# One transformer block on one core: all eight late chunks of the modulation matrix summed by TensorE matvecs

## The chip, the cores and the metric

The kernel runs on one core of a Trainium2 chip. Five engines run their own instruction streams in order and meet by semaphores: TensorE (PE, with its weight loads shown as PEld), VectorE (DVE), ScalarE (ACT), GpSimd (POOL) and SyncE (SP), which here issues the transfers between HBM and SBUF. The metric is the device time of one execution in microseconds (us).

## The reference

One block on 256 tokens of width 1024: a modulation vector from `c`, a mixer (a gated delta rule with four heads and a chunked attention with eight), and a mixture of 32 experts, four per token.

```python
mod = jax.nn.silu(c) @ w_ada[l] + b_ada[l]                       # [1, 6*1024]
sh1, sc1, ga1, sh2, sc2, ga2 = [m[:, None, :] for m in jnp.split(mod, 6, axis=-1)]
h = rms_norm(x, norm_w[l, 0]) * (1 + sc1) + sh1
y = hybrid_mixer(h, w_in[l], ...)                                # delta rule, attention, w_out
x = x + ga1 * rms_norm(y, norm_w[l, 1])
h = rms_norm(x, norm_w[l, 2]) * (1 + sc2) + sh2
y = moe_ffn(h, w_router[l], b_router[l], w_up[l], b_up[l], w_down[l], b_down[l])
x = x + ga2 * rms_norm(y, norm_w[l, 3])
```

`w_ada` is 1024 x 6144. The change concerns the product of `silu(c)` with the columns of it that give `ga1`, `sh2`, `sc2` and `ga2`.

## The kernel before

**Stages.** The front stage (0 to about 254 us in the trace) computes the modulation, the projections, the delta rule, the attention, the output projection, the residual and the routing. The expert stage then goes through 14 groups of one, two or four experts; each group loads six blocks of 512 columns per expert (2 MB each) and multiplies them by gathered tokens. The weights of the experts are 402 MB and come through a ring of ten slots in SBUF (`wB`, `w0`, `wC`, `wE`, `w1`, `wD`, `wF`, `wh`, `wA`, `wx`). In the front stage the same memory holds the projection weights, the pieces of the delta rule and the late chunks.

**The modulation.** `w_ada` is cut in twelve chunks of 512 columns, each [128 partitions, 8 k, 512]. Four chunks (`sc1`, `sh1`) come first (`hpath`). The other eight are the late chunks: chunk i belongs to segment i // 2 (0 `ga1`, 1 `sh2`, 2 `sc2`, 3 `ga2`), half i % 2. `ADAPOS` says after which step of the work a chunk is loaded and reduced, `ADATAG` in which slot (`wF` or `wB`); in program order they are c0, c2, c4, c3, c6, c1, c5, c7 (c1 and c5 at the same step, c7 a step later). `ADA` holds a letter per chunk.

With "D" (six chunks: c0, c1, c3, c4, c6, c7) VectorE multiplies the eight k slices by `silu(c)` and adds them in place (L723 once, L725 seven times, 512 wide), and four matmuls against a column of ones (L728) sum over the partitions. With "P" (c2 and c5) TensorE does it all in `colvec`: eight matmuls whose stationary operand is one value of `silu(c)` per partition, spread over 32 columns (L196); four of them fill the four groups of 32 rows of a PSUM bank, the next four add to them. ScalarE copies the bank to SBUF (`ev`, L199), and four matmuls against the indicator `ind` (L201) sum the four groups. Either way VectorE then adds bias and norm weight (L733, L736). Both ways take a PSUM bank of the tag `tp`, of which there are two, shared with the transposes of the attention (L785) and others.

**What sets the order.** The source lists the work once; a scheduler orders each engine's instructions when the kernel is built, with the delta rule (`chain`, L486) marked as high priority, so a change of one line can move instructions on every engine. From L1043 on the order on TensorE and VectorE is as written. On SyncE the transfers go one after the other: one that waits holds all behind it.

**The delta rule.** `chain` inverts triangular blocks by five levels (L595 in `pair_mm`): a product, copies of it to SBUF (L626 on ScalarE, L627 on VectorE), two more products, subtractions on VectorE (L633, L637), and so on. Then come the joining of the two halves (L659, L662), and the passing of the state (L684 to L709), each step a few matmuls and copies (L654, L680). `level` (L586) makes the masks that the levels need; the first two are on VectorE (L588). The projections run in the order k, q, qb, kb, vb, v, z, each in two column halves of two heads (`stream`, L406). A column half needs its weight split in a rounded part and a rest (`split`, L205): ScalarE rounds (L217), VectorE and GpSimd subtract (L219, L222); TensorE then runs 24 matmuls of 256 columns per head (L232).

**After the front stage.** `delta_out` normalizes the delta rule's result (L884 squares on ScalarE, L888 on VectorE), L891 transposes it, and the output projection, the residual, the routing and the first gather follow.

Of the kernel before, what the change touches and what calls it, by code (L numbers as in the profile page):

```python
# [24 lines left out]
K2 = 4  # L25
K1 = 6
KV = 2
ADA = list("DDPDDPDD")
ADATAG = list("FFBFFFFB")
ADAPOS = [5, 31, 6, 12, 8, 31, 19, 32]  # L30
ADABANK = "tp"
# [18 lines left out]
def block_kernel(ctx, tc, x, small, rows, rel_ext, wpre, wexp, b_up, b_down, out,  # L50
# [22 lines left out]
    def bank(tag="mm"):  # L73
        return ps.tile([P, 512], F32, tag=tag, bufs=PB[tag], name=tag)
# [641 lines left out]
    def modrow(seg, hf, w):  # L716

        if ADA[2 * seg + hf] == "P":
            b_ = bank("tp")
# [682 lines left out]
```

## Time and profile before

| | |
|---|---|
| median of 3 runs | 1191.61 us (1190.53 to 1195.18) |
| profiled execution | 1192.22 us, span 1190.4 us |
| PE, DVE, ACT, POOL busy | 1029.8, 358.7, 190.3, 104.1 us |
| granted TensorE clock, mean | 0.953 |
| HBM read | 449.50 MB, 379 GB/s over the span |

In the tables of stretches each row gives the busy time of the engines in that stretch with the number of instructions, the granted clock of TensorE (1.00 is 2.4 GHz, 0.50 is 1.2 GHz), the busy share of the 16 DMA engines and the GB/s. In rows in order of time stand the start, the duration, the engine, the line, the operation and the tiles written and read; a bracket at the end gives the idle time of the engine before it and who ended it. TensorE's fp32 matmuls appear as two records each, those of the rounded type as one.

### The profile page before, as it was taken

What the parts mean: (1) busy time and instruction counts of PE and PEld (TensorE: products, weight loads), DVE (VectorE), ACT (ScalarE), POOL (GpSimd) and SP (SyncE); (2) the same over time, 40 slices, a digit from 0 to 9 for tenths busy, and PEclk for the clock granted to TensorE, in tenths of its full rate; (3) what the DMA queues carried; (4) which work ended last, traced back from release to release, by engine and by line L of the source; (5) the groups of instructions that cost most, each with busy time, mean ns of one, the idle gap of its engine ahead of it and who ended that gap; (6) DMA issues with size and microseconds to landing.
All of it is one profiled execution on the core that took longest, in us unless ns stands there. A gap on an engine that the chain in (4) does not pass through costs nothing. (4 is left out here: it accounts for less than half of the span.)

```text
span 1190.4 us, 14727 instructions
## 1 busy us (share of the span) xinstructions
PE 1029.8 (87%) x5845; PEld 495.3 (42%) x5845; DVE 358.7 (30%) x851; ACT 190.3 (16%) x380; POOL 104.1 (9%) x91
## 2 busy tenths in 40 slices
PE   4898999899977789999976788989967698998985
PEld 2697998654321224435421233335322142433331
DVE  5387888654103022122111012122201011111113
ACT  3453327331001001011000001011001001010101
POOL 1557514200000000000000000000000000000001
PEclk9899999989998999999997999999988899999998
DMA  9925346989999999999999999999999999999993
GB/s 362 403 81 213 142 178 237 401 353 386 421 421 422 421 408 426 423 428 423 423 422 424 427 425 426 424 427 425 420 426 425 423 427 423 426 426 422 428 419 149
DMA packets 51463, 451.93 MB, mean 380 GB/s; under 512 B 5760, under 2 KB 7424, under 8 KB 9408
## 3 DMA queue, kind: packets, MB, share of 16 engines
q1 hardware_dynamic: 51392, 450.97, 91.3%
q8 instruction: 47, 0.77, 0.3%
q14 instruction: 24, 0.20, 0.0%
HBM read 449.50 MB, written 1.05 MB: 379 GB/s over the span
## 5 line engine op out<-in xcount | busy, mean ns | idle before, releaser
L1123 PE MATMUL dl<-w_f,xg 128*64 128x512 f32 (+1 forms) x224 | 113.5, 653 | 9.7 <-DMA w_f<-in_wexp_dram 9.7
L1177 DVE TENSOR_TENSOR acc<-acc,mm 128x512 f32<-128x512 f32 x52 | 35.8, 688 | 242.2 <-PE mm L1172 242.2
L1123 PE MATMUL mm<-w_f,xg 128*64 128x512 f32 (+2 forms) x208 | 92.7, 594 | 4.0 <-DMA w_f<-in_wexp_dram 4.0
L1279 POOL TENSOR_TENSOR wF_f<-acc,m_row 128x512 f32<-128x512 f32 x3 | 3.8, 1273 | 943.1 <-DMA w_f<-in_wexp_dram 937.3
L1123 PE MATMUL dl<-wh,xg 128*64 128x512 f32 (+2 forms) x144 | 70.3, 633 | 5.1 <-DMA wh<-in_wexp_dram 5.1
L1123 PE MATMUL dl<-wD_f,xg 128*64 128x512 f32 (+1 forms) x128 | 65.4, 662 | 4.3 <-DMA wD_f<-in_wexp_dram 4.3
L1172 PE MATMUL mm<-yg,wts 128*128 128x512 f32 x112 | 54.5, 614 | 11.0 <-ACT yg L1169 10.0
L1141 ACT ACTIVATE sg<-gm 128x512 f32<-128x512 f32 x28 | 17.6, 630 | 288.9 <-DVE gm L1139 263.1
L1123 PE MATMUL dl<-wE_f,xg 128*64 128x512 f32 (+2 forms) x112 | 55.2, 645 | 6.4 <-DMA wE_f<-in_wexp_dram 6.4
L1123 PE MATMUL mm<-wB_f,xg 128*64 128x512 f32 (+2 forms) x128 | 57.6, 595 | 0.0
L1123 PE MATMUL mm<-wh,xg 128*64 128x512 f32 (+1 forms) x144 | 57.1, 594 | 0.5 <-DMA wh<-in_wexp_dram 0.5
L1123 PE MATMUL dl<-wF_f,xg 128*64 128x512 f32 (+2 forms) x112 | 54.5, 628 | 2.8 <-DMA wF_f<-in_wexp_dram 2.8
L1123 PE MATMUL dl<-wC_f,xg 128*64 128x512 f32 (+2 forms) x112 | 55.4, 638 | 1.4 <-DMA wC_f<-in_wexp_dram 1.4
L1003 PEld LDWEIGHTS tp<-oh,x 128*128 128x128 f32 x432 | 50.7, 192 | 13.2 <-issue 11.4
L1003 PE MATMUL tp<-oh,x 128*128 128x128 f32 x432 | 54.8, 279 | 0.7 <-ACT aT__3377 L1152 0.7
L1123 PE MATMUL mm<-wE_f,xg 128*64 128x512 f32 (+1 forms) x112 | 49.6, 595 | 3.9 <-DMA wE_f<-in_wexp_dram 3.9
L1169 ACT COPY yg<-dl 128x512 f32<-128x512 f32 x27 | 15.8, 585 | 224.8 <-PE dl L1123 224.8
L1123 PE MATMUL dl<-wB_f,xg 128*32 128x512 f32 (+1 forms) x96 | 47.7, 634 | 3.5 <-DMA wB_f<-in_wexp_dram 3.5
L1013 DVE TENSOR_SCALAR xg<-tp,mc,mc 128x128 f32<-128x128 f32 x52 | 19.6, 405 | 101.1 <-PE dl L1123 92.4
L1123 PE MATMUL mm<-wC_f,xg 128*64 128x512 f32 (+1 forms) x112 | 50.0, 594 | 0.0
L1123 PEld LDWEIGHTS dl<-w_f,xg 128*64 128x64 f32 (+1 forms) x224 | 28.2, 134 | 42.6 <-issue 25.7
L1139 DVE TENSOR_SCALAR gm<-dl 128x512 f32<-128x512 f32 x14 | 9.7, 692 | 119.5 <-PE dl L1134 119.5
(640 smaller groups left out, 2193.3 us busy)
## 6 DMA issues: line engine op xcount, KB each, us to landing
wh<-in_wexp_dram SPq DMA_DIRECT2D x57, 1024.0 KB, 24.7
w_f<-in_wexp_dram SPq DMA_DIRECT2D x26, 2048.0 KB, 26.1
wA_f<-in_wexp_dram SPq DMA_DIRECT2D x36, 1024.0 KB, 22.2
wF_f<-in_wexp_dram SPq DMA_DIRECT2D x36, 1024.0 KB, 29.7
wE_f<-in_wexp_dram SPq DMA_DIRECT2D x15, 2048.0 KB, 29.4
wC_f<-in_wexp_dram SPq DMA_DIRECT2D x15, 2048.0 KB, 27.0
wB_f<-in_wexp_dram SPq DMA_DIRECT2D x13, 2048.0 KB, 22.2
wD_f<-in_wexp_dram SPq DMA_DIRECT2D x13, 2048.0 KB, 34.2
```

The costliest lines, as they stand in the source:

```text
L1003: T.matmul(b_[:, k * 128:(k + 1) * 128], x2[:, a, half(n)][:, k * 128:(k + 1) * 128], oh[:, a], start=a == tiles[0], stop=a == tiles[-1])
L1013: V.tensor_scalar(xg[:, k], src, mc, sc, op0=ALU.mult, op1=ALU.add)
L1123: T.matmul(b_[i * n:(i + 1) * n, :], lhs[:, k, i * n:(i + 1) * n], w(k), start=k == 0, stop=last and k == 7)
L1139: V.tensor_scalar(gm, bs[0], 7.0, None, op0=ALU.min)
L1141: S.activation(sg, gm, AF.Sigmoid, scale=1.702)
L1169: S.copy(yg, b_)
L1172: T.matmul(cb, wt[:, a], yg, start=True, stop=True)
L1177: V.tensor_add(acc[:, a, sl], acc[:, a, sl], cb)
L1279: (V if a and n else G).tensor_mul(fin[:, 0, a, sl], acc[:, a, sl], m3_row[:, sl])
```

## The change

`ADA` becomes all "P". The six chunks that VectorE summed now go through `colvec` as c2 and c5 do. Nothing else is edited.

```diff
-ADA = list("DDPDDPDD")
+ADA = list("PPPPPPPP")
```

The branch that reads it (unchanged):

```python
if ADA[2 * seg + hf] == "P":
    b_ = bank("tp")
    colvec(w, csil, b_, ADABANK)
else:
    ac = w[:, 0, :]
    V.tensor_scalar(ac, ac, csil[:, 0:1], None, op0=ALU.mult)
    for k in range(1, 8):
        V.scalar_tensor_tensor(ac, w[:, k, :], csil[:, k:k + 1], ac, op0=ALU.mult, op1=ALU.add)
    b_ = bank("tp")
    for m in range(4):
        T.matmul(b_[:, m:m + 1], ac[:, m * 128:(m + 1) * 128], ones[:, 0:1], start=True, stop=True)
```

The order of the instructions moves in three places that matter below.

On VectorE, where the delta rule's first masks are made (L588; L580 makes their input, L219 are subtractions of weight splits, L723 and L725 a chunk's sum, L733 and L736 a chunk's last step), the order before is:

```order
L580 TENSOR_TENSOR wB_f<-wE_f 64x512 x2
L219 TENSOR_TENSOR w_r<-w_f,wh 128x512
L588 TENSOR_TENSOR Lm<-wB_f,lvm_249 128x512
L588 TENSOR_TENSOR Lm<-wB_f,lvm_258 128x512
L576 SCALAR_TENSOR_TENSOR wE_f<-dl,bb,m_incT 128x128 x4
L617 TENSOR_TENSOR wB_f<-id_231,Lm 128x512
L723 TENSOR_SCALAR wF_f<-wF_f,csil 128x512
L725 SCALAR_TENSOR_TENSOR wF_f<-wF_f,csil 128x512
L621 TENSOR_TENSOR wE_f<-id_231,dl 64x8x64 x2
```

and in the changed kernel:

```order
L580 TENSOR_TENSOR wB_f<-wE_f 64x512 x2
L733 SCALAR_TENSOR_TENSOR mc_946<-tp,sm 128x4
L733 SCALAR_TENSOR_TENSOR mc_1025<-tp,sm 128x4
L736 SCALAR_TENSOR_TENSOR mc_1025<-mc_1025,sm 128x4
L219 TENSOR_TENSOR w_r<-w_f,wh 128x512
L219 TENSOR_TENSOR w_r<-w_f,whx 128x512
L219 TENSOR_TENSOR w_r<-w_f,wh 128x512
L588 TENSOR_TENSOR Lm<-wB_f,lvm_249 128x512
L588 TENSOR_TENSOR Lm<-wB_f,lvm_258 128x512
L617 TENSOR_TENSOR wB_f<-id_231,Lm 128x512
```

The two masks now stand behind the last steps of c2 and c4 and behind the splits of the last three projection halves.

On TensorE, at the last levels of the delta rule (L595) and the joining of its halves (L659, L662; L232 with `wA_r` are projections, L761 the attention's scores, L785 its transposes), the order before is:

```order
L595 MATMUL dl<-wB_f 64x64 x24
L761 MATMUL mm<-wC_f 128x256 x2
L232 MATMUL mm<-wh,wA_r 128x256 x16
L232 MATMUL mm<-w_r,wA_r 128x256
L595 MATMUL dl<-wB_f 64x64 x8
L659 MATMUL dl<-wE_f 64x64 x8
L232 MATMUL mm<-w_r,wA_r 128x256 x7
L761 MATMUL mm<-wC_f 128x256 x4
L785 MATMUL tp<-ident,w_f 128x128 x4
L662 MATMUL dl<-wB_f 64x64 x4
L785 MATMUL tp<-ident,w_f 128x128 x3
L662 MATMUL dl<-wB_f 64x64 x4
```

and in the changed kernel, with L606 and L610 two transposes of the same chain:

```order
L761 MATMUL mm<-wC_f 128x256 x4
L595 MATMUL dl<-wB_f 64x64 x32
L606 MATMUL dl<-ident,kqT 128x128 x4
L610 MATMUL dl<-ident,wB_f 128x128 x4
L595 MATMUL dl<-wE_f,Lm 64x64 x16
L595 MATMUL dl<-wB_f 64x64 x32
L659 MATMUL dl<-wE_f 64x64 x8
L662 MATMUL dl<-wB_f 64x64 x8
L684 MATMUL dl<-wE_f 128x128 x4
L688 MATMUL dl<-wE_f,wB_f 128x128 x4
L692 MATMUL dl<-wE_f 128x128 x4
L696 MATMUL dl<-wE_f,kdt 128x128 x4
```

The projections and the attention's transposes no longer stand between the steps; the row goes on with L700, L703, L707 and L709, and the transposes (L785) begin behind them.

On TensorE, at the end of the first half of the output projection (L232 with `wC_r`) and ahead of L891, the order before is:

```order
L232 MATMUL mm<-wh,wC_r 128x512 x8
L232 MATMUL mm<-w_r,wC_r 128x512 x4
L196 MATMUL tp<-wF_f,csil 32x512 x8
L201 MATMUL tp<-ind,ev 128x1 x4
L728 MATMUL tp<-ones,wB_f 128x1 x4
L891 MATMUL tp<-ident,wE_f 128x128 x8
```

and in the changed kernel:

```order
L232 MATMUL mm<-w_r,wC_r 128x512 x4
L196 MATMUL tp<-wF_f,csil 32x512 x8
L201 MATMUL tp<-ind,ev 128x1 x4
L196 MATMUL tp<-wB_f,csil 32x512 x8
L201 MATMUL tp<-ind,ev 128x1
L891 MATMUL tp<-ident,wE_f 128x128 x4
L201 MATMUL tp<-ind,ev 128x1 x3
```

The sum of c7 (slot `wB`) is now eight matvecs with a copy behind them, in the place of the four matmuls against ones.

## Rows read from the trace of the kernel before

**Rows 1.** The page's 40 slices of the span, busy in tenths: three lines.
```profile
PE   4898999899977789999976788989967698998985
DVE  5387888654103022122111012122201011111113
DMA  9925346989999999999999999999999999999993
```

**Rows 2.** Stretches: length, PE, PEld, DVE, ACT, POOL busy, PEclk, DMA, GB/s.
```profile
87.50:112.00 24.50, 24.00 (x227) 22.28 (x226) 16.32 (x35) 12.00 (x19) 14.57 (x11) 1.00 0.46 172
112.00:124.00 12.00, 8.09 (x65) 7.48 (x63) 11.77 (x10) 3.01 (x4) 10.81 (x7) 0.72 0.48 176
124.00:172.00 48.00, 47.85 (x616) 46.17 (x616) 41.04 (x68) 10.77 (x18) 15.59 (x12) 1.00 0.42 155
172.00:204.00 32.00, 31.07 (x319) 26.57 (x318) 24.63 (x45) 20.25 (x61) 14.33 (x12) 1.00 0.67 264
...
215.20:221.20 6.00, 3.86 (x33) 2.27 (x32) 5.79 (x14) 0.74 (x2) 2.57 (x2) 0.98 1.03 419
...
290.00:1170.00 880.00, 766.64 (x3694) 286.77 (x3693) 149.81 (x313) 75.38 (x147) 0.00 (x0) 0.96 1.01 423
```

**Rows 3.** SyncE's waits, 180 to 300 us: waited for, total, times, longest.
```profile
SPq L1115 <- PE mm L1123: 17.4, 1, 17.4
SPq L81 <- PE tp L728: 12.9, 1, 12.9
```

**Rows 4.** The same columns as Rows 2, the stretch in which the ring was full.
```profile
260.00:262.00 2.00, 2.00 (x12) 0.78 (x13) 0.00 (x0) 0.40 (x1) 0.00 (x0) 1.00 0.00 0
```

**Rows 5.** SyncE in order of time: the load of c5.
```profile
205.14 0.33 SPq L81 DMA_DIRECT2D wF_f<-in_wpre_dram  x1
```

**Rows 6.** TensorE in order of time: c2, then the end of c5 and c7.
```profile
100.62 1.92 PE L196 MATMUL tp<-wB_f,csil 128*32 128x512 f32 x16
102.47 2.17 PE L232 MATMUL mm<-wA_r,wh 128*128 128x256 f32 x16
...
107.25 0.50 PE L201 MATMUL tp<-ind,ev 128*128 128x1 f32 x4
...
217.82 1.05 PE L201 MATMUL tp<-ind,ev 128*128 128x1 f32 x8 [0.71 <-ACT ev L199]
218.73 1.03 PE L728 MATMUL tp<-ones,wB_f 128*128 128x1 f32 x8
```

**Rows 7.** VectorE by line, 87.5 to 221 us: busy, mean ns, idle before.
```profile
L725 DVE SCALAR_TENSOR_TENSOR wF_f<-wF_f,csil 128x512 f32<-128x512 f32 x31 | 31.9, 1028 | 0.5
L633 DVE TENSOR_TENSOR wE_f<-wE_f,dl 64x512 f32<-64x512 f32 x10 | 6.8, 684 | 3.3 <-PE dl L595 3.1
...
L725 DVE SCALAR_TENSOR_TENSOR wB_f<-wB_f,csil 128x512 f32<-128x512 f32 x7 | 5.2, 743 | 0.0
...
L627 DVE COPY wB_f<-dl 64x512 f32<-64x512 f32 x5 | 3.5, 695 | 1.0 <-PE dl L595 0.8
...
L680 DVE COPY wE_f<-dl 128x256 f32<-128x256 f32 x2 | 0.8, 410 | 0.0
```

**Rows 8.** TensorE in order of time: its waits for VectorE.
```profile
108.24 1.15 PE L595 MATMUL dl<-id,Lm 64*64 64x64 f32 x32 [0.49 <-DVE Lm L588]
...
116.39 2.69 PE L595 MATMUL dl<-wE_f,Lm 64*64 64x64 f32 x32 [3.73 <-DVE wE_f L621]
...
193.63 1.16 PE L696 MATMUL dl<-wE_f,kdt 128*128 128x128 f32 x8 [0.93 <-DVE wE_f L680]
...
221.26 1.97 PE L891 MATMUL tp<-ident,wE_f 128*128 128x128 f32 x8 [1.49 <-DVE mc L733]
```

**Rows 9.** VectorE in order of time: work that stands beside the chain.
```profile
174.73 1.29 DVE L766 TENSOR_TENSOR w_f<-mm,strip 128x512 f32<-128x512 f32 x2 [0.22 <-PE mm L761]
...
199.87 1.22 DVE L219 TENSOR_TENSOR w_r<-w_f,wh 128x1024 fp32r<-128x1024 f32 x1 [4.22 <-ACT wh L217]
```

**Rows 10.** ScalarE in order of time: one of the squares of L884.
```profile
201.25 0.30 ACT L884 ACTIVATE junk<-wE_f 128x128 f32<-128x128 f32 x1
```

## The prediction

> **What bounds the kernel now.** I read the slices of the page first. From the third to the seventh slice VectorE is at 7 or 8 tenths, TensorE at 8 or 9, and the DMA engines have holes; from the tenth on the DMA engines are full and VectorE is at 5 tenths or less [rows 1]. So there are two regimes. From 290 to 1170 us the share of DMA is 1.01 and TensorE has 113 us of slack in 880 [rows 2]: the stream of expert weights is the limit, and nothing that the change touches runs there. What the front stage costs shifts this stream as a whole: SyncE waited 17.4 us in one piece for the first expert group's matmuls to free a slot [rows 3], and for two microseconds nothing was transferred [rows 4]. The ring is full when the experts begin, so a front stage that ends later by some microseconds ends the kernel later by as many. An earlier one gains the same, as long as the loads are there.
>
> Then the front stage. By stretches TensorE is busy 24.00 of 24.50, 8.09 of 12, 47.85 of 48 and 31.07 of 32 us; VectorE 16.32, 11.77, 41.04 and 24.63 [rows 2]. Both are heavily used, but the one without slack is TensorE. Its order holds the projections, into which the delta rule's steps are laid, and what it waits for shows when VectorE decides: 0.49 us for the masks, 3.73 for L621, 0.93 in the passing of the state, 1.49 for L733 of c7 [rows 8]. That is where removing VectorE work can pay.
>
> **What goes.** The six chunks' sums are 8 operations each; those in `wF` after 87.5 us run at a mean of 1028 ns, the seven of c7 at 743 [rows 7], together 37.1 us of VectorE. On the path they are worth the waits they caused: 3.73 + 0.49 + 1.49 = 5.7 us. The wait of 0.93 is for the chain's own copy and stays. The wait of 3.73 was followed by a clock of 0.72 in the mean over 112 to 124 us [rows 2], and 32 records of L595 took 2.69 us there against 1.15 at full clock [rows 8]; another 1.5 us that should go with the wait. Bounds of what goes: nothing (if VectorE is late for its own reasons) and 7.2.
>
> **What comes.** Eight matvecs in column groups hold TensorE from 100.62 to the next matmul at 102.47, 1.85 us [rows 6]; six times that is 11.1. The closing matmuls are an even swap: 1.05 us for eight records of L201, 1.03 for L728 [rows 6]. ScalarE gets six copies; it is busy 10.77 of 48 us in the longest stretch [rows 2], so they hide, except where the matmuls that need the copy follow at once. For c5 the trace has that: 0.71 us; for c2, with matmuls in between, L201 at 107.25 shows no wait [rows 6]. In the new order c0, c4, c3 and c1 have matmuls in between, c6 has the rest of the chain, and c7 now follows c5 directly ahead of L891: one more wait, 0.7 us. The Trainium skill (TensorEngine Tiling (Array Packing), PSUM Bottleneck) says that column tiling speeds up TensorE but not the evacuation of PSUM, which may become the bound. If all six copies showed, they would cost 6 x 0.71 = 4.3 us in place of 0.7 and the sum would be 14.9 in place of 11.3; the trace disagrees for c2 and agrees for c5 [rows 6].
>
> **What moves.** The masks L588 now stand behind three weight splits, the last of which needs a ScalarE rounding into a buffer that the projections must free first. On TensorE the first L595 comes 145 projection matmuls later (9 of kb, 96 of vb, 40 of v), some 19 us by 2.17 us for 16 [rows 6]. That by itself costs nothing: the projections have to run anyway. But the chain's end then has none left to cover it. From the second last level on the steps follow one another, and each waits for VectorE or ScalarE. What stands on these engines between two steps: for two levels a copy of 0.695 and two subtractions of 0.684 [rows 7], 4.1 us; four softmax operations of 512 columns in VectorE's order, at 1.29 for two, 2.6; two subtractions of 1024 columns at 1.22 [rows 9], 2.4; five copies of 0.41 [rows 7], 2.1; four squares of ScalarE of 0.30 ahead of a copy [rows 10], 1.2. Together 12.4 us if none of it is covered. The lowest end is what these steps cost before, 0.93 [rows 8]. Between them I take the middle, 6.7: transposes of the same chain and the second halves of the products still lie beside some of it, and no row is nearer.
>
> Where the work is moved from matters as well: the attention's transposes, its last products and the output projection now come behind the chain, and so do the matvecs of c1. SyncE's load of c5 into `wF` waits for c1 to be read (12.9 us before) [rows 3] and is issued at 205.14 [rows 5]; behind it in the queue stand nearly all expert loads. It shifts with TensorE, so the transfers gain nothing from the earlier loads.
>
> **The sum.** 11.1 + 0.7 + 6.7 - 5.7 - 1.5 = 11.3 us on the profiled execution's 1192.22 (span 1190.4 and 1.8 around it), which is 1203.5. That execution lies 0.6 above the median of the runs, so I predict 1203. With the ends of the unknowns: 11.1 + 0.7 + 0.9 - 7.2 = 5.5 and 11.1 + 0.7 + 12.4 = 24.2, the clock apart.
>
> **Rivals.**
> First, the chain stays covered. TensorE's own steps and the transposes fill the waits, as before, and only 0.93 us shows: +5.5, which is 1197. For it: in 172 to 204 us TensorE was busy 31.07 of 32 while the same steps ran [rows 2]. Against it: that was with projections and transposes between them.
>
> Second, not slower: VectorE is the pace. TensorE's busy time has modelled ends, so it may contain short waits for VectorE that no row shows; VectorE was busy 11.77 of 12 and 41.04 of 48 us where the chain ran [rows 2]. If its 37.1 us less let the chain go fast enough that the six matvecs fall into such hidden time, their 11.1 us vanish and the 7.2 us remain as gain, less the 0.7: 6.5 us faster, 1185. It decides from the point where matmuls that need no VectorE result follow one another slower than 2.17 us for 16 in the stretch from 124 to 172 us. Against it: 616 records in 47.85 us [rows 2], and projections there have no one to wait for.
>
> Third, the clock falls in the uncovered end of the chain. After the 3.73 us wait the clock fell and L595 took 2.69 in place of 1.15 us; after waits of 0.71 and 1.49 [rows 6, 8] eight records of L891 took 1.97 where eight of L696 took 1.16 [rows 8]. The last level and the joining are 128 records of L595 and its like, and seven steps like L696 follow; all at half clock they cost 4 x 1.54 + 7 x 0.81 = 11.8 us more: 1215. The Trainium skill (TensorE: Matmul & The Clock Gate, A second HAM failure mode: psum-queue depth-cycling) describes such a case: short idle times between groups of matmuls, frequent enough, let the clock go back and forth between its two levels. The rows agree that it falls after such waits; whether waits of about a microsecond in a row suffice, no row of this stretch shows, since it had no such waits.
>
> That the change does not do what it says can be left aside: in the new order L723, L725 and L728 are gone.
>
> **Chances.** About 0.5% (6 us, 1185.6 to 1197.6) is what a measurement of this kernel can tell from no change. The forecast has 0.48, of which 0.05 end below 1197.6; the covered chain 0.24, three quarters of it within 0.5%; the fallen clock 0.15, slower; the pace of VectorE 0.13, of which 0.09 beyond -0.5%. Together slower 0.64, within 0.27, faster 0.09. The range from 1189 to 1216 leaves out the best of the second rival and the upper part of the third; the likeliest case alone spans 1197 to 1209.
>
> **What would show it.** Right: six L196 groups between 95 and 225 us at 1.85 us each; the first L595 near 133 us (108.24, 19 for the projections and 5.6 for three more chunks); waits of TensorE for VectorE or ScalarE that add up to 4 to 10 us between the last projection and L709; L891 and the first expert matmul (L1123) later by about 11 us, and the same shift at 290 us and at the end; the share of DMA from then on unchanged. Wrong: L709 followed at once by a full row of work and an end within 6 us of before (first rival); no wait in the chain and L1123 earlier than before (second); a clock of 0.50 over ten microseconds around the chain's end (third). A shift at L1123 that does not reach the end would refute the reading that the stream passes it on.

## The result and the profile after

The changed kernel takes 1204.26 us (median, 1203.21 to 1204.81), 1.0104 of the kernel before, interval [1.0091, 1.0117]: slower by 12.6 us, 1.3 us over the forecast. Its profiled span is 1202.0 us (1190.4 before). The first expert matmul (L1123) starts at 265.51 us in place of 253.53, 12.0 later; what lies behind it is as long as before (936.5 us to the end of the span, 936.9 before).

The page of the changed kernel, 40 slices of its span as in [rows 1], in tenths:

```profile
PE   4799999989977889999986888999976699998995
DVE  5473664273113012121211012121211011111113
PEclk9999997989998899999996999999988799999998
DMA  9927443698999999999999999999999999999994
```

VectorE's third to seventh slices fall from 8, 7, 8, 8, 8 tenths to 7, 3, 6, 6, 4, and TensorE's third to eighth stand at 9. The stretches in the changed kernel, which answer to [rows 2] (length, then busy us and instructions of PE, PEld, DVE, ACT, POOL, granted clock, DMA share, GB/s):

```profile
112.00:124.00 12.00, 12.00 (x103) 12.00 (x102) 2.75 (x4) 5.00 (x6) 6.38 (x6) 1.00 0.77 325
124.00:172.00 48.00, 48.00 (x613) 41.69 (x612) 33.15 (x54) 12.46 (x35) 17.25 (x15) 1.00 0.42 155
176.00:178.00 2.00, 0.92 (x15) 0.80 (x13) 1.94 (x4) 1.59 (x5) 0.26 (x1) 0.96 1.00 422
178.00:198.00 20.00, 19.07 (x164) 18.24 (x163) 9.36 (x16) 6.39 (x11) 7.05 (x6) 0.50 0.33 136
198.00:204.00 6.00, 5.55 (x48) 5.36 (x48) 1.93 (x10) 2.97 (x12) 0.00 (x0) 0.97 0.94 350
290.00:1170.00 880.00, 775.85 (x3714) 288.41 (x3711) 154.72 (x331) 75.61 (x147) 0.00 (x0) 0.95 1.01 423
```

From 112 to 172 us TensorE has neither a wait nor a slow clock. Then comes the row to read twice: from 178 to 198 us it is busy 19.07 us at a clock of 0.50. The kernel before was busy for just as long in the same stretch, at full clock:

```profile
178.00:198.00 20.00, 19.07 (x168) 15.77 (x168) 16.97 (x32) 12.44 (x39) 11.05 (x9) 1.00 0.67 265
```

Busy time alone hides the difference. TensorE's rows around it, in the changed kernel (start, us, engine, line; the bracket is the wait ahead and its releaser), which answer to [rows 6, 8]:

```profile
130.82 0.86 PE L595 MATMUL dl<-id,Lm 64*64 64x64 f32 x22
153.23 1.90 PE L196 MATMUL tp<-wF_f,csil 128*32 128x512 f32 x10
157.06 1.06 PE L196 MATMUL tp<-wF_f,csil 128*32 128x512 f32 x6
177.20 1.47 PE L595 MATMUL dl<-wB_f 64*64 64x64 f32 x16 [1.08 <-DVE wE_f L633]
183.56 5.37 PE L595 MATMUL dl<-wB_f 64*64 64x64 f32 x58
191.05 1.97 PE L662 MATMUL dl<-wB_f 64*64 64x64 f32 x16 [0.47 <-ACT wB_f L653]
193.48 2.08 PE L684 MATMUL dl<-wE_f 128*128 128x128 f32 x8 [0.47 <-ACT wE_f L653]
198.55 1.06 PE L696 MATMUL dl<-wE_f,kdt 128*128 128x128 f32 x8
202.74 0.71 PE L709 MATMUL dl<-vn,wE_f 128*128 128x128 f32 x4 [0.45 <-ACT vn L680]
214.87 1.04 PE L196 MATMUL tp<-wF_f,csil 128*32 128x512 f32 x2
216.86 1.92 PE L196 MATMUL tp<-wF_f,csil 128*32 128x512 f32 x14
228.03 1.92 PE L196 MATMUL tp<-wF_f,csil 128*32 128x512 f32 x16
230.66 1.05 PE L201 MATMUL tp<-ind,ev 128*128 128x1 f32 x8 [0.71 <-ACT ev L199]
234.27 0.38 PE L201 MATMUL tp<-ind,ev 128*128 128x1 f32 x2 [0.71 <-ACT ev L199]
234.52 0.63 PE L891 MATMUL tp<-ident,wE_f 128*128 128x128 f32 x4
265.51 0.64 PE L1123 MATMUL mm<-wB_f,xg 128*64 128x512 f32 x1
```

The chain's end waits little: 1.08 + 0.47 + 0.47 + 0.45 = 2.5 us. But behind the 1.08 the clock falls, and eight records of L684 take 2.08 us, while L696, of the same shape, takes 1.06 as soon as the clock is back.

Two of the six new matvecs do not stand as one block. Other matmuls part c6's after 10 of its 16 records (153.23 to 155.06, then 157.06 to 158.05) and c1's after 2 (214.87 to 215.84, then 216.86 to 218.71). Each of these two holds TensorE for 2.82 us in place of 1.85.

An account of TensorE, to be used below, cuts a stretch in slices of 1 us: idle time; busy time x (1 - granted clock), called clock loss; the rest, called work. It is mine, worked out from the rows of the stretches. From 87.5 us to L891:

| us | length | idle | clock loss | work |
|---|---|---|---|---|
| before | 133.76 | 8.3 | 2.8 | 122.6 |
| changed | 147.02 | 4.8 | 9.8 | 132.4 |
| difference | +13.3 | -3.5 | +7.0 | +9.8 |

From L891 to L1123 it gave 1.3 back (32.27 to 30.99; clock loss 5.8 to 2.9).

Two cautions. The window does not begin at the same point of the work: L562 starts at 89.07 us in the kernel before and at 86.16 in the changed one (between these two in every other run but e4), so some 2.0 us of L562, L571 and L232 are counted before and not in the changed kernel, and 0.8 us of its closing matmuls stand behind L891. By the starts of the rows L196 alone holds TensorE for 16.9 us in place of 3.8, which is 13.1 more. And the columns are not independent: while the clock is low, a matmul fills time in which TensorE might else wait.

### The profile page after: what moved, and what is told of

Same layout as the page of the kernel before. It is cut to its first block, busy times and chain, and to the rows that moved or that the text cites. A ratio compares the mean times of both kernels' runs of the same rounds, so it can differ in the third digit from the quotient of the medians.

```text
span 1202.0 us, 14892 instructions
## 1 busy us (share of the span) xinstructions
PE 1050.6 (87%) x5941; PEld 498.9 (42%) x5941; DVE 316.4 (26%) x803; ACT 194.1 (16%) x386; POOL 99.3 (8%) x91
## 5 line engine op out<-in xcount | busy, mean ns | idle before, releaser
L1123 PE MATMUL dl<-w_f,xg 128*64 128x512 f32 (+1 forms) x224 | 111.0, 640 | 8.8 <-DMA w_f<-in_wexp_dram 8.8
L1123 PE MATMUL mm<-w_f,xg 128*64 128x512 f32 (+2 forms) x208 | 94.2, 603 | 2.8 <-DMA w_f<-in_wexp_dram 2.8
L1123 PE MATMUL dl<-wh,xg 128*64 128x512 f32 (+2 forms) x144 | 68.5, 619 | 5.4 <-DMA wh<-in_wexp_dram 5.4
L1123 PE MATMUL dl<-wD_f,xg 128*64 128x512 f32 (+1 forms) x128 | 62.9, 640 | 4.4 <-DMA wD_f<-in_wexp_dram 4.4
L1123 PE MATMUL mm<-wB_f,xg 128*64 128x512 f32 (+2 forms) x128 | 59.3, 610 | 0.0
L1123 PE MATMUL dl<-wE_f,xg 128*64 128x512 f32 (+2 forms) x112 | 52.9, 623 | 6.5 <-DMA wE_f<-in_wexp_dram 6.5
L1123 PE MATMUL dl<-wF_f,xg 128*64 128x512 f32 (+2 forms) x112 | 54.3, 625 | 2.9 <-DMA wF_f<-in_wexp_dram 2.8
L1123 PE MATMUL mm<-wh,xg 128*64 128x512 f32 (+1 forms) x144 | 56.8, 594 | 0.0
L1123 PE MATMUL dl<-wC_f,xg 128*64 128x512 f32 (+2 forms) x112 | 53.0, 616 | 2.0 <-DMA wC_f<-in_wexp_dram 1.8
L1123 PE MATMUL mm<-wE_f,xg 128*64 128x512 f32 (+1 forms) x112 | 51.3, 611 | 2.5 <-DMA wE_f<-in_wexp_dram 2.5
L1123 PE MATMUL mm<-wC_f,xg 128*64 128x512 f32 (+1 forms) x112 | 51.5, 611 | 0.0
L1123 PE MATMUL dl<-wB_f,xg 128*32 128x512 f32 (+1 forms) x96 | 46.8, 626 | 2.9 <-DMA wB_f<-in_wexp_dram 2.9
L1011 ACT ACTIVATE xg<-tp,mc,mc 128x128 f32<-128x128 f32 x52 | 21.8, 454 | 147.8 <-DVE xg L1013 147.8
L1123 PEld LDWEIGHTS dl<-w_f,xg 128*64 128x64 f32 (+1 forms) x224 | 27.5, 131 | 36.8 <-issue 20.8
```

What stands on the lines that cost most here:

```text
L1011: S.activation(xg[:, k], src, AF.Identity, scale=mc, bias=sc)
L1123: T.matmul(b_[i * n:(i + 1) * n, :], lhs[:, k, i * n:(i + 1) * n], w(k), start=k == 0, stop=last and k == 7)
```

## The experiments

All kernels are edits of the two, timed against the kernel before on the same chip (1192.45 us beside e1 to e4, 1191.83 beside e5 to e8, 1191.66 beside e9 to e12; differences below are to these). The ratio stands with its interval; L891 and L1123 are starts in the one profiled execution (221.26 and 253.53 before). Single executions scatter: e9 and e10 below are the same program up to 228 us, and L709 starts at 206.35 in the one and at 203.86 in the other. So landmarks are good to 2 or 3 us, and small differences are left to the ratios. The profiled execution of e2 and that of e5 are the slowest of their four (2.4 and 1.9 us above the median), that of e10 the fastest of its twelve (2.8 below). Where added lines shift the numbers, L891 and L1123 stand for the same statements.

| | what is on TensorE | median us | ratio | L891 | L1123 |
|---|---|---|---|---|---|
| changed | all eight | 1204.26 | 1.0104 [1.0091, 1.0117] | 234.52 | 265.51 |
| e1 | c2, c5, c3 | 1203.95 | 1.0095 [1.0079, 1.0110] | 230.05 | 265.06 |
| e2 | all, c3 later | 1204.33 | 1.0100 [1.0084, 1.0115] | 234.72 | 266.45 |
| e3 | all, half sums | 1201.17 | 1.0075 [1.0062, 1.0089] | 228.03 | 260.76 |
| e4 | none | 1209.33 | 1.0141 [1.0126, 1.0157] | 237.31 | 270.57 |
| e5 | all, fill in the chain | 1203.65 | 1.0091 [1.0076, 1.0105] | 231.10 | 263.38 |
| e6 | c2, c5, c0 | 1198.72 | 1.0054 [1.0042, 1.0067] | 225.12 | 258.40 |
| e7 | c2, c5, c7 | 1191.86 | 1.0001 [0.9992, 1.0010] | 222.64 | 253.47 |
| e8 | c2, c5, c4 | 1192.80 | 1.0006 [0.9995, 1.0016] | 219.24 | 253.29 |
| e9 | c2, c5, c4, c7 | 1193.47 | 1.0011 [1.0001, 1.0020] | 222.12 | 254.05 |
| e10 | as e9, fill in the routing | 1191.93 | 1.0002 [0.9990, 1.0013] | 219.64 | 250.44 |
| e11 | c2, c5, fill in the routing | 1191.93 | 1.0000 [0.9991, 1.0009] | 219.27 | 253.35 |
| e12 | c2, c5, each four times | 1199.83 | 1.0066 [1.0054, 1.0079] | 228.33 | 261.10 |

**The matvecs' own time: e12 and e3.** My theory was that it passes to the end; the rival, that waits take it up.

e12 adds such work to the kernel before and takes none from VectorE. The scheduler's order of VectorE changes with it all the same: c4's first five operations (L723 and four of L725) now stand ahead of the masks L588.

```diff
-        for k in range(8):
+        for k in list(range(8)) * reps:      # reps = 4 for c2 and c5
```

> The kernel before, with the eight L196 matmuls of c2 and of c5 done four times in a row (their sums are four times too large, which changes the values of mc for c2 and c5): 6 x 1.85 = 11.1 us of TensorE, the work of the changed kernel's six matvecs, with VectorE's work and the delta rule's place (356 projection matmuls ahead) left as before. If that work passes to the end in full: 1202 to 1204 us, L1123 at 264 to 265. If the waits for VectorE take part of it up (3.73 and 1.49 us, and the half clock behind them): 1195 to 1199 us.

Measured: +8.2 us, between the two ranges (2 us under the one, 1 over the other). The two groups grew by 10.3 us, not by 11.1: to 7.01 for c2 (98.64 to 105.65) and 7.07 for c5, from 1.85 and 1.92. Some four fifths come through. The waits moved more than they went: TensorE waits 4.65 us for the first mask (0.49 before), and no longer for L621 (3.73 before) or ahead of L891 (1.49 before). The last row is VectorE's:

```profile
98.64 7.07 PE L196 MATMUL tp<-wB_f,csil 128*32 128x512 f32 x64
116.72 1.97 PE L595 MATMUL dl<-id,Lm 64*64 64x64 f32 x32 [4.65 <-DVE Lm L588]
115.03 3.19 DVE L588 TENSOR_TENSOR Lm<-wB_f,lvm 128x512 f32<-128x512 f32 x2
```

e3 takes half of it away from the changed kernel:

```diff
-        for k in range(8):
+        for k in range(ks):                      # ks = 4 for the late chunks
...
-                     start=k < 4, stop=k >= 4)
+                     start=k < 4, stop=k >= ks - 4)
```

> The changed kernel with four in place of eight L196 matmuls per late chunk, so half of each sum is left out; chain late as in the changed kernel (506 projection matmuls ahead of the first L595, 112 behind the last). If TensorE's time in the matvecs passes to the end one to one: 8 x 0.93 = 7.4 us less than the changed kernel, 1196 to 1198 us, at L1123 as well. If the matvecs lie in time that is lost anyway (chain or clock decide): at most 2 us less, 1202 to 1204 us. The half clock around 180 to 200 us stays in both.

Measured: 3 to 4 us less than the changed kernel (3.1 between the medians, 3.9 by the differences to the kernel before), 4.8 at L1123: between the two ranges. Half a matvec is more than half the time, 1.00 of 1.85 (here c0's, up to the next matmul). As c6's now stands as one block, L196 holds TensorE for 9.1 us in all in place of 16.9, so 7.8 went:

```profile
96.57 1.06 PE L196 MATMUL tp<-wF_f,csil 128*32 128x512 f32 x8
97.57 2.18 PE L232 MATMUL mm<-wA_r,wh 128*128 128x256 f32 x16
```

Two fifths to a half of the work removed comes back as time, four fifths of the work added in e12 shows as time. By these shares the 13.1 us of L196 are worth some 5 to 10 of the 12.6.

**The place of the chain: e1 and e2.** The rest I put down to the delta rule standing late. One letter moves it, c3's, with a sixth of the work:

```diff
-ADA = list("DDPDDPDD")
+ADA = list("DDPPDPDD")
```

> Only c3 goes to TensorE; c0, c4, c6, c1 and c7 stay on VectorE. One matvec is added (1.85 us), but the order of the delta rule becomes about that of the changed kernel: the first L595 stands behind 515 projection matmuls (351 before, 496 in the changed kernel) and 112 matmuls of its last steps behind the last projection. If the late, uncovered chain with its half clock is what costs: L1123 later by 6 to 11 us, 1198 to 1203 us, a clock of 0.50 over ten microseconds or more around 180 to 205 us. If the matvecs' own time is what costs: 1.85 less what a wait or two gives back, 1190 to 1194 us.

Measured: 1203.95, a microsecond over the range of the late chain and ten over that of the work. But the clock is 0.50 only in pieces, and waits count as much. From 87.5 us to L891 the account reads idle 12.0, clock loss 7.1, work 123.5 (before: 8.3, 2.8, 122.6). Two of its waits, on TensorE:

```profile
118.06 1.84 PE L728 MATMUL tp<-ones,wF_f 128*128 128x1 f32 x8 [4.61 <-issue]
228.33 1.86 PE L728 MATMUL tp<-ones,wB_f 128*128 128x1 f32 x8 [3.96 <-DVE wB_f L725]
```

The profile names no releaser for the first. But its matmuls read c4's sum, and the last four operations of that sum on VectorE end at 117.95:

```profile
113.95 4.00 DVE L725 SCALAR_TENSOR_TENSOR wF_f<-wF_f,csil 128x512 f32<-128x512 f32 x4
```

The second is for c7's sum on VectorE. So both are waits for VectorE's own sums. The order that one chunk brings about can cost some ten microseconds beside its 1.85 of work.

e2 does the opposite, all eight matvecs with the chain early:

```diff
-ADAPOS = [5, 31, 6, 12, 8, 31, 19, 32]
+ADAPOS = [5, 31, 6, 17, 8, 31, 19, 32]
```

> All eight chunks on TensorE as in the changed kernel, but c3 is loaded and summed at step 17 in place of 12; by that alone the delta rule stands early again (385 projection matmuls ahead of the first L595, 4 matmuls of 64 columns behind the last projection). Late chain and its half clock as the cost: only the work stays, 11.1 + 0.7 - 5.7 - 1.5 = 4.6 us over the kernel before, 1194 to 1199 us, clock 1.00 from 124 to 200 us. Matvecs' own time as the cost: as the changed kernel, 1203 to 1206 us.

Measured: 1204.33, the number of the other theory, and 5 us above mine. My theory of the place falls as it stood: with the chain early, TensorE runs from 124 to 188 us at full clock, and loses time by other waits right behind. TensorE's rows and stretches in e2:

```profile
192.03 0.71 PE L703 MATMUL dl<-wE_f,kdt 128*128 128x128 f32 x4 [2.83 <-ACT wE_f L680]
200.85 1.05 PE L201 MATMUL tp<-ind,ev 128*128 128x1 f32 x8 [0.70 <-ACT ev L199]
204.59 1.09 PE L785 MATMUL tp<-ident,w_f 128*128 128x128 f32 x4 [2.19 <-DVE rso1x L138]
```

```profile
192.00:196.00 4.00, 3.96 (x23) 3.97 (x24) 1.05 (x4) 1.67 (x6) 4.00 (x4) 0.64 1.04 432
203.00:210.00 7.00, 5.41 (x28) 4.12 (x29) 4.59 (x23) 1.77 (x4) 0.43 (x1) 0.52 0.52 225
```

In this order too all of the attention's transposes (L785) stand behind the chain; the kernel before had laid 16 of the 24 between its last steps. Its account to L891: idle 7.7, clock loss 4.5, work 135.0. What an order costs is read from its waits; the late place is only one way to make some.

**Nothing on TensorE: e4.**

```diff
-ADA = list("DDPDDPDD")
+ADA = list("DDDDDDDD")
```

> The other way: c2 and c5 go to VectorE too, no late chunk on TensorE. TensorE loses 2 x 1.85 us and the exposed copy of 0.71, VectorE gains 16 operations of about 1.03 us. If TensorE's time decides: 1187 to 1189 us. If VectorE's waits grow instead (16 us more in stretches in which it is busy 11.77 of 12 and 41 of 48 us): 1192 to 1200 us.

Measured: +16.9 us, more than either range. TensorE waits 2.10 and 2.60 us for VectorE (L355, the sums of the short convolution) already at 74 and 86 us, 4.82 at L595, and 9.86 at the end of the front stage for c5's sum, which VectorE does in turn with c7's:

```profile
121.97 3.31 PE L595 MATMUL dl<-wB_f 64*64 64x64 f32 x42 [4.82 <-DVE wB_f L627]
233.88 1.86 PE L728 MATMUL tp<-ones,wF_f 128*128 128x1 f32 x8 [9.86 <-DVE wF_f L725]
```

The kernel before lies between two losses: all eight chunks on either engine cost time.

**The clock in the chain's end: e5.** A fill keeps TensorE at work in the last two levels:

```diff
+            if s_ >= 4:
+                T.matmul(bank("tp"), ident, Ti, start=True, stop=True)
             yield 0.9
             ub = pair_mm(Ti, X)
...
+            if s_ >= 4:
+                for z_ in range(2):
+                    T.matmul(bank("tp"), ident, X, start=True, stop=True)
```

> The changed kernel with six more matmuls of 512 columns in the last two levels of the delta rule (one behind the first product, two behind the third; results unused), to keep TensorE at work there; the order is else that of the changed kernel but for single rows. One such fp32 matmul is about 0.9 us (eight of a quarter of the columns, L196, take 1.85), 5.4 us in all. If short waits and thin work let the clock fall from 178 to 198 us: it stays at 1.00 for half or more of that stretch, 5 to 9 us come back, 1199 to 1205 us. If the clock there has another cause: half clock as before, the fill itself at half clock, 1209 to 1215 us.

Measured: 1203.65, within the range of the first theory; but that range holds the changed kernel's 1204.26 too, so the time alone decides little. The clock decides: it stays at 1.00 here, and its mean over an execution is 0.955 to 0.965 in the four of e5, 0.946 to 0.954 in the four of the changed kernel. Of the chain's waits two of 0.47 and 0.45 remain. In e5:

```profile
178.00:198.00 20.00, 19.50 (x214) 15.36 (x212) 9.54 (x16) 7.11 (x15) 7.58 (x6) 1.00 0.60 238
```

Six matmuls more, and L891 starts 3.4 us earlier than in the changed kernel. That more work on TensorE holds the clock there is shown. Which part of it does is not told apart: the fill closes the 1.08 us wait and lies in the short ones, and c6's matvec has moved into the chain's end too, to 188.89 us. The end shows little of the gain: 0.6 us between the medians, with intervals that overlap. 1.3 us go in the routing, where the half clock now lasts from 248 to 261 us (256 to 262 in the changed kernel). From L1123 to the end the profiled execution takes 940.3 us, 3.8 more than the changed kernel's; in the other thirteen profiles, before and after among them, it is 936.0 to 938.5. Whether that is the scatter of one execution or something that the fill does, these runs can't tell.

**One chunk at a time: e6, e7, e8.**

```diff
-ADA = list("DDPDDPDD")
+ADA = list("PDPDDPDD")      # e6: c0
+ADA = list("DDPDDPDP")      # e7: c7
+ADA = list("DDPDPPDD")      # e8: c4
```

> Only c0 goes to TensorE (delta rule at its early place, 353 projection matmuls ahead of the first L595). In the kernel before c0 is summed between 80 and 90 us, ahead of all waits; now c4's first operation stands ahead of the masks. Prices per chunk add up: 1.85 us more, 1193 to 1195 us. Price set by the waits of the place: the 3.73 us wait stays (c4 still stands near L621) and nothing is freed, 1193 to 1198 us; faster than 1191 us only if the waits for VectorE behind c0 go.

Measured: +6.9 us, just over the upper end of the range by waits. The waits ahead of L595 (1.45 for the masks, 5.35 for L621) and of L891 (2.55, for c7) all grew: 0.49, 3.73 and 1.49 before [rows 8].

> Only c7 goes to TensorE; nothing changes ahead of 205 us. Costs 1.85 us and an exposed copy of 0.71, frees the 1.49 us wait for L733 ahead of L891: net +1.1 us. By prices of the place: L891 0 to 2 us later, 1191 to 1194 us. By an equal share of what the changed kernel lost (12.7 / 6): 1194 to 1195 us.

Measured: +0.0, the place's price, not an equal share.

> Only c4 goes to TensorE. In the kernel before its operations stand between L617 and L621 on VectorE, where TensorE then waits 3.73 us and the clock falls. Price of the place: 1.85 us more, 3.73 us of wait and up to 3.5 us of half clock less, with the first L595 some 34 projection matmuls later: 1187 to 1190 us. Price of the work alone: 1193 to 1195 us. If the later chain meets waits as with c3: 1198 us or more.

Measured: +1.0 us, with an interval that holds none, just under the price of the work and far from the gain that I had from the place. Both waits of [rows 8] at the chain's start are gone (two of 0.92 and 2.37 come later), and L891 starts 2 us earlier, but now waits for c7:

```profile
219.24 1.97 PE L891 MATMUL tp<-ident,wE_f 128*128 128x128 f32 x8 [2.56 <-DVE mc L733]
```

Behind this wait the clock is low, and the way to L1123 takes 34.05 us in place of 32.27. One chunk of 1.85 us thus costs 0, 1, 7 or 11.5 us (e7, e8, e6, e1): its price goes with the waits that its place makes and the low clock behind them. By the account e1 has 3.7 us more idle time and 4.3 more clock loss than the kernel before, e6 2.0 and 2.1 (10.4 and 4.9).

**Towards a faster version: e9, e10, e11.** e9 takes the 2.56 away as well:

```diff
-ADA = list("DDPDDPDD")
+ADA = list("DDPDPPDP")
```

> c4 and c7 go to TensorE. c4 alone brought L891 forward to 219.24 us (221.26 before) but left it behind a wait of 2.56 us for c7's sum; c7 alone shortened the way from L891 to L1123 from 32.27 to 30.83 us. If the waits of the place decide: the 2.56 goes, 1.85 + 0.71 comes, L891 at 219 to 220, L1123 at 250 to 251, 1188 to 1190 us. If prices of single chunks simply add: 1192 to 1194 us.

Measured: 1193.47, in the range in which single prices add up (0 and 1.0; +1.8). Two copies show behind c5 and c7, 0.71 and 0.70, in the place of that wait. e10 and e11 add a fill in the routing, to e9 and to the kernel before:

```diff
+        fb = bank("dl")
+
+        def fill(n):
+            for _ in range(n):
+                T.matmul(fb, onesb, onesb[:, None, :].to_broadcast([P, 4, P]), start=True, stop=True)
+
+        fill(3)                              # ahead of x2_trans(0, n)
...
+        fill(6)                              # ahead of the norms that x2_trans(1, n) needs
```

> As the kernel with c4 and c7 on TensorE, and nine bf16 matmuls of 512 columns (results unused) in the routing, three ahead of the first transposes of x and six ahead of the second, to keep TensorE at work through waits of 0.76 and 1.73 us, behind which the clock is 0.50 in all kernels so far. If the clock falls by those waits and the half clock delays the routing: clock 1.00 there, 2 to 5 us less than without the fill, 1184 to 1188 us. If VectorE's short operations set the pace of the routing: 0 to 1 us more than without the fill.

> The kernel before with the same nine matmuls in the routing and nothing else. Half clock stood from 241 to 251 us there and cost TensorE about 5 us. If the fill keeps the clock: 2 to 5 us less, 1187 to 1190 us. If VectorE sets the pace: 1191.5 to 1193 us.

Measured: in e10 the clock is 1.00 through the routing (0.53 in e9 from 242 to 253 us), and L891 to L1123 takes 30.80 us (31.93 in e9). So the 4.5 us of clock loss that e9 has there are worth 1.1 of time: the fill takes a part, and TensorE now waits for VectorE where it did not in e9, 0.57 us ahead of L1123 and 1.49 ahead of L966 in the routing (a row of e10):

```profile
246.52 0.18 PE L966 MATMUL dl<-mk,strib 128*128 128x32 bf16 x1 [1.49 <-DVE mk L953]
```

In e11 the clock had fallen already behind the wait at L891, ahead of the fill, and fell again. The stretches of e10, e9 and e11, in that order:

```profile
228.00:250.00 22.00, 18.30 (x145) 13.70 (x143) 17.41 (x75) 11.18 (x33) 1.28 (x1) 1.00 1.01 427
```

```profile
242.00:253.00 11.00, 9.51 (x61) 7.87 (x62) 9.11 (x42) 6.05 (x19) 0.00 (x0) 0.53 1.00 424
```

```profile
218.00:225.00 7.00, 5.73 (x19) 4.59 (x20) 2.99 (x8) 1.76 (x3) 0.73 (x1) 0.52 0.98 419
246.00:252.00 6.00, 5.33 (x32) 4.94 (x32) 5.10 (x25) 3.20 (x10) 0.00 (x0) 0.50 0.98 418
```

In time e11 is in the range of VectorE's pace, though the mean clock over its twelve executions is 0.954, against 0.951 in the kernel before. e10 is in neither: 1.5 us below e9 in the medians, with intervals that overlap, and 4 us above the hoped-for range. No version beat the kernel before.

## Why the prediction was right

The time came out 1.3 us from the forecast. Of the working behind it the bound and what goes held, the new work and the place held in kind, and the waits of the chain's end did not.

**The bound: right.** L1123 is 12.0 us later, the span 11.6, with DMA share 1.01 and 423 GB/s in between as before; SyncE's long wait for the first expert group is 16.8 us (17.4 in [rows 3]). In e1 to e4 the shift at L1123 (11.5, 12.9, 7.2, 17.0) returns in the span as well (11.9, 14.5, 7.8, 17.2).

**What goes: right.** The three waits of 5.7 us and the low clock at 116 us are gone. The low clock was under-sized: 1.5 by one pair of rows, 2.8 by the account.

**What comes: right in kind, the work too small.** Four of the six new L196 groups hold TensorE for 1.85 to 1.92 us, the two that are parted for 2.82 each: 13.1 in place of 11.1. Two copies show, at c5 and c7, 0.71 each. The Trainium skill (TensorEngine Tiling (Array Packing), PSUM Bottleneck) has the copy out of PSUM as the possible bound once the matmuls run side by side; here it showed at two of the eight chunks, as the forecast had it, and at three in e2.

**What moves: the place right, the size wrong.** The first L595 is at 130.82 (133 forecast) and nothing covers the chain's end. But the term "Between them I take the middle, 6.7" is the step that failed: 2.5 us of waits were measured, where the prediction's own sign of being right was 4 to 10. In all, TensorE's waits from 87.5 us to L891 are 4.8 us; the sum's terms make 8.3 - 5.7 + 0.7 + 6.7 = 10.0.

**In its place: the third rival's mechanism.** The clock at 0.50 for twenty microseconds, which the prediction named as the mark of that rival and as a sign of being wrong, is there, and costs 9.8 us by the account where it had 11.8. It came not through many waits of a microsecond but through one of 1.08 and three of less than half. The Trainium skill (TensorE: Matmul & The Clock Gate, A second HAM failure mode: psum-queue depth-cycling) describes a clock that goes to and fro with short idle times between groups of matmuls; the rows agree that one of 1.08 us can be enough, but here it fell once and stayed down. In e3 the same steps run at full clock for some microseconds longer, and show what the low clock hides:

```profile
173.97 1.14 PE L595 MATMUL dl<-wB_f 64*64 64x64 f32 x16 [1.04 <-DVE wE_f L633]
178.00 1.14 PE L595 MATMUL dl<-wE_f,Lm 64*64 64x64 f32 x16 [0.67 <-ACT wB_f L626]
180.63 4.11 PE L595 MATMUL dl<-wB_f 64*64 64x64 f32 x45 [0.25 <-DVE wB_f L627]
```

The waits of 0.67 and 0.25 are not there in the changed kernel. With them the chain's end of e3 waits 3.4 us, which is still under the 6.7.

So the total was met by luck, by errors that offset each other. By the account: waits 5.2 us too large, clock loss 8.5 too small (7.0 more in place of 1.5 less), work 1.3 too large (9.8 for 11.1), and 1.3 came back in the routing: 0.7 in all, from 11.3 to 12.0 at L1123. The matvecs themselves were put 2.0 too small; the account's 9.8 lies below their 13.1 mostly by the unlike ends of its window. Of the sum the waits that go and the second copy were right in size and for their reason, and the work in kind: e12 shows that 10.3 us of it, at the early place, come through as 8.2.

**The other rivals.** VectorE as the pace is refuted by the result, which is slower, and by e12 and e3: more matvec work is more time, less is less. Neither passes in full, so a part of that work does fall into time that is lost anyway. (Its 37.1 us are L725 alone; L723 adds 3.5 in the same window, on which nothing hangs.) The covered chain (1197) was not built by the change. e2 came near to it in place, and lost as much by other waits.

What stays open: why e2 and the changed kernel lose equally much by different waits, why e5's gain at L891 does not reach the end, and what decides whether the clock falls behind a wait.

## What to carry to other kernels

Between two engines that are both nearly full, the price of an operation is not its duration but the waits that its place in the order makes: one chunk of 1.85 us cost between 0 and 11.5 here. Read busy time and granted clock together: 19.07 us of 20 can be full speed or half of it. A total that comes out right proves no term; only the rows of each term do.

## What the runs showed of the hardware

The granted clock fell in or behind single waits of 1.08 us (changed kernel, for 20 us), 1.73 (routing), 2.19 and 2.83 (e2), 3.73 (before). It did not fall behind the 0.71 waits at 230.66 and 234.27 us in the changed kernel. The length of the wait alone does not decide, and neither do TensorE's rows ahead of it. The kernel before and e7 have the same rows up to one wait of 0.68 us; the same nine records behind it take 2.34 us at a clock of 1.00 in the one and 3.91 at 0.57 in the other:

```profile
206.80 2.34 PE L232 MATMUL mm<-wh,wC_r 128*128 128x512 f32 x9 [0.68 <-ACT wC_r L805]
206.17 3.91 PE L232 MATMUL mm<-wh,wC_r 128*128 128x512 f32 x9 [0.68 <-ACT wC_r L805]
```

So it is with e8 (first two rows) and e10, also alike up to there: twelve records of L232 take 1.67 us behind a wait of 2.37, and 2.91 behind the same wait of 2.20:

```profile
150.28 1.14 PE L595 MATMUL dl<-wB_f 64*64 64x64 f32 x16 [2.37 <-DVE wE_f L633]
151.76 1.67 PE L232 MATMUL mm<-wA_r,whx 128*128 128x256 f32 x12
150.07 1.14 PE L595 MATMUL dl<-wB_f 64*64 64x64 f32 x16 [2.20 <-DVE wE_f L633]
151.58 2.91 PE L232 MATMUL mm<-wA_r,whx 128*128 128x256 f32 x12
```

One profile of a kernel therefore does not show where its clock falls in every execution.

Eight column-group matmuls in one block hold TensorE for 1.85 us and four for 1.00: the second four are cheaper than the first. One matmul of them alone takes as long as four, 0.97 us (c1's first, 214.87 to 215.84), so a group that other matmuls part costs 2.82.
